# The recurrence's middle chunks beside other projections, and the diagonal layer's products in order of time

## The chip, the core and the metric

One Trainium2 chip, one of its cores. The metric is the device time of one execution in microseconds (us). Engines: TensorE (PE, with its weight loads PEld), VectorE (DVE), ScalarE (ACT), GpSimd (POOL) and SyncE (SP), whose one queue issues all DMAs of this kernel. Each engine takes its instructions in the order in which they stand in its queue.

## The reference

Two layers over two token groups, 128 context tokens and 2048 sample tokens, with D = 1024. All is float32. The first layer has two mixers side by side: a gated linear recurrence in four heads (HGRN2), in both directions, and a complex diagonal state space (S5) of 32 groups, also in both directions:

```
z = jnp.dot(h, w_in)                       # h: normalised and modulated tokens, 1024 -> 3584
q, f_fw, f_bw, v, g_a, u, g_b = jnp.split(z, EVEN_SPLITS, axis=-1)
S_t = diag(f_t) S_{t-1} + k_t v_t^T        # HGRN2, per head, forward and backward
o_t = S_t^T q_t
x_t = lbar * x_{t-1} + bb u_t              # S5, per group, forward and backward
y   = gelu(y_f + y_b + d_skip * u)
y   = y * sigmoid(y @ w_glu + b_glu)
out = concat(norm(o) * silu(g_a), y * silu(g_b)) @ w_out
```

The second layer is a gated short convolution between two projections. The outputs are all tokens after a last norm and the final states of the first layer.

## The kernel before

Tokens stand in the free dimension. They are cut into six tiles (five of 384, the last of 256) and these into three parts, `p0`, `p1` and `p2`, of two tiles each. A projection (`proj_all`, `proj_group`, `mm3`, L361) multiplies a 128x128 block of weights with a tile's `h`. Each operand is split into a high and a low half (`whi`, `wlo`, `hhi`, `hlo`), so one block takes 8 x 3 = 24 matmul passes into a PSUM tile `pj`. `load_w` loads a block by DMA, ACT casts it (L341), and DVE or POOL, in turns, makes `wlo` (L345). `make_h` norms a tile and writes its two halves; of these there are three pairs of buffers. `spill` evacuates `pj` and stores it to HBM: `zq`, `zff`, `zfb`, `zv` (from `qfv()`, the recurrence's inputs) and `zga`, `zgb` (from `gates()`).

The diagonal layer handles 16 tokens at a time: 136 blocks of 16 for 2176 tokens. `spill_u` stores its input to `u_d`; `s5_load_u` loads it as `su`, 128 partitions by 272 elements per group: for each block of 16 tokens two neighbouring elements, one for each half `hh`. `s5_in` (L602) multiplies `su` with the input matrices `psi`, which it first makes on DVE and POOL from loaded tables `pe` and `pb`, and copies the result (PSUM tile `lv`) into the state array `X` (L637, L638). `X` does not lie in order of time: block `c = 8 a + b` stands in group `b` at place `a`, so that `s5_scan` can run over 8 groups of 17. `s5_out` (L694) takes `X` out again (`sxm`, L711 and L712), builds its output matrices (`SO`, and `GS`, which goes through HBM and returns as `sM`) and accumulates in `lv`: `sM` with `su` (L717, L719) and `SO` with `sxm` (L722). Before, all these products have their columns in the order of `X`: the operand `su` is read as 8 runs of 17 at a step of 16 elements.

The recurrence handles chunks of 128 tokens, 17 of them. `hgrn_chunk` is a generator: it loads `hq`, `hff`, `hvf`, goes through seven levels of doubling blocks (products at L796, L820 and L822; decays on DVE and POOL at L826 and L828) and then updates the state `S` (L850 to L882). `hgrn_run` starts a chunk every 4 steps and so keeps three or so alive. Modulation rows (`mod_late`, L225) are issued beside them.

The program is put into order when it is built: a scheduler takes instructions by rank, the rank being the place in the program's text, and by when it reckons an operand to be ready. `rank(tc, n)` shifts the rank of what stands under it: a negative `n` puts it earlier. The result is a fixed order for each engine. Before, the second `hgrn_run` (chunks 6 to 11) stands ahead of `gates()` for `p1`, and `make_h` of both tiles of `p2` behind it.

Of the kernel before, what the change touches and what calls it, by code (L numbers as in the profile page):

```python
# [15 lines left out]
AF = mybir.ActivationFunctionType  # L16
OP = mybir.AluOpType
# [10 lines left out]
NC8 = NTOK // 8  # L28
NSAM = DEC // 8
NC16 = NTOK // 16  # L30
NS16 = DEC // 16
NG16 = NC16 // 8
# [17 lines left out]
MWB = 3  # L50
RX = 0
FU = 2
KPOOL = (1, 2, 4, 6)

PV = {}
# [8 lines left out]
def vw(t, off, dims):  # L64
    return bass.AP(t.tensor, t.offset + off, [list(t.ap[0])] + [list(d) for d in dims])


def raw_ap(t, off, dims):
    return bass.AP(t.tensor, t.offset + off, [list(d) for d in dims])
# [525 lines left out]
def s5_load_u(nc, g, p, g0):  # L595
    u = p.tile([128, 2, NC8], F32, name="su")
    for j in range(2):
        nc.sync.dma_start(u[:, j], raw_ap(g.u_d, (g0 + j) * 16 * 8 * NC8, [(NC8, 8), (8 * NC8, 16), (1, NC8)]))
    return u


def s5_in(nc, g, p, X):  # L602

    V, A, T, G = nc.vector, nc.scalar, nc.tensor, nc.gpsimd
    W = WX
    for r in range(8):
        G0 = 4 * r
        us = [s5_load_u(nc, g, p, G0 + 2 * q) for q in range(2)]
        SI = []
        for d in range(2):  # L610
            bt = p.tile([128, 2, 4, 2, 64], F32, name="pb", bufs=1)
            nc.sync.dma_start(bt.rearrange("p a g r q -> p a (g r q)"),
                              raw_ap(g.I["s5_bt"], d * 16 * 8192 + r * 1024, [(0, 8), (8192, 16), (1, 1024)]))
            for hh in range(2):
                e = p.tile([128, 4, 2, 64], F32, name="pe")
                nc.sync.dma_start(e.rearrange("p g r q -> p g (r q)"),
                                  raw_ap(g.et_d, ((d * 16 + 8 * (1 - hh)) * 32 + G0) * 128,
                                         [(32 * 128, 8), (0, 16), (1, 512)]))
                si = p.tile([128, 4, 2, 64], F32, name=f"psi{d}{hh}")
                tb = p.tile([128, 4, 2, 64], F32, name="ptb")  # L620
                V.tensor_tensor(si, vw(e, 0, [(128, 4), (0, 2), (1, 64)]), bt[:, 0], op=OP.mult)
                G.tensor_tensor(tb, vw(e, 64, [(128, 4), (0, 2), (1, 64)]), bt[:, 1], op=OP.mult)  # L622
                V.tensor_tensor(si[:, :, 0], si[:, :, 0], tb[:, :, 0], op=OP.subtract)
                V.tensor_tensor(si[:, :, 1], si[:, :, 1], tb[:, :, 1], op=OP.add)
                SI.append(si)
        for q in range(2):
            pr = 2 * r + q
            for j in range(2):
                P = g.ps_l.tile([128, 512], F32, name="lv")
                for d in range(2):  # L630
                    for hh in range(2):
                        T.matmul(out=P[:, d * NC16:(d + 1) * NC16],  # L632
                                 lhsT=SI[2 * d + hh][:, 2 * q + j].rearrange("p r q -> p (r q)"),
                                 rhs=vw(us[q], j * NC8 + hh, [(2, 8), (16, NG16)]), start=(hh == 0), stop=(hh == 1))
                o = slice(64 * j, 64 * j + 64)
                Pv = P[:, :2 * NC16].rearrange("p (d c) -> p d c", d=2)
                A.activation(vw(X[o], pr * W + NG16, [(32 * W - NG16, 2), (1, NC16)]), Pv[0:64], AF.Copy)  # L637
                V.tensor_copy(vw(X[o], (16 + pr) * W + NG16, [(32 * W - NG16, 2), (1, NC16)]), Pv[64:128])  # L638


def s5_powers(nc, g, p):
# [52 lines left out]
def s5_out(nc, g, p, X):  # L694
    V, A, T, G = nc.vector, nc.scalar, nc.tensor, nc.gpsimd
    W = WX
    todo = [s5_matrices(nc, g, p, pr) for pr in range(AH)]
    for pr in range(16):
        g0 = 2 * pr
        if pr + AH < 16:  # L700
            todo.append(s5_matrices(nc, g, p, pr + AH))
        so = todo.pop(0)
        u = s5_load_u(nc, g, p, g0)
        M = p.tile([128, 2, 384], F32, name="sM")
        for j in range(2):
            nc.sync.dma_start(M[:, j], raw_ap(g.gs_d, (g0 + j) * 16 * 496, [(16, 8), (496, 16), (1, 384)]))
        for j in range(2):
            gr = g0 + j
            o = slice(64 * j, 64 * j + 64)
            xm = p.tile([128, 2, NC16], F32, name="sxm")  # L710
            V.tensor_copy(xm[0:64], vw(X[o], pr * W, [(32 * W + NG16, 2), (1, NC16)]))  # L711
            A.activation(xm[64:128], vw(X[o], (16 + pr) * W, [(32 * W + NG16, 2), (1, NC16)]), AF.Copy)  # L712
            P = g.ps_l.tile([128, 512], F32, name="lv")
            for hh in range(2):
                po = P[:, hh * NC16:(hh + 1) * NC16]
                ue = [vw(u, j * NC8 + i, [(2, 8), (16, NG16)]) for i in range(2)]
                T.matmul(out=po, lhsT=M[:, j, 128:256], rhs=ue[hh], start=True, stop=False)  # L717
                c0 = 0 if hh == 0 else 256
                T.matmul(out=po, lhsT=M[:, j, c0:c0 + 128], rhs=ue[1 - hh], start=False, stop=False)  # L719
                for d in range(2):  # L720
                    e = 8 * hh + 1 - d
                    T.matmul(out=po, lhsT=so[d][:, j, e:e + 8].rearrange("p e o -> p (e o)"), rhs=xm[:, d],  # L722
                             start=False, stop=(d == 1))
            z = p.tile([128, NC8], F32, name="sz")
            y = p.tile([128, NC8], F32, name="sy")
            Pv = P[:, :NC8]
            A.activation(z, Pv, AF.Square)
            c2 = 2.0 * math.sqrt(2.0 / math.pi)
            V.tensor_scalar(z, z, 0.044715 * c2, c2, op0=OP.mult, op1=OP.add)
            V.tensor_tensor(z, z, Pv, op=OP.mult)  # L730
            A.activation(z, z, AF.Sigmoid)
            V.tensor_tensor(vw(y, 0, [(1, 2), (2, 8), (16, NG16)]), z.rearrange("p (h b a) -> p h b a", h=2, b=8),
                            Pv.rearrange("p (h b a) -> p h b a", h=2, b=8), op=OP.mult)
            nc.sync.dma_start(g.y_d[gr * 16:gr * 16 + 16].rearrange("o t c -> t o c"), y)


# [2 lines left out]
def hgrn_run(nc, g, cs, every, end=False):  # L739

    todo, t = list(cs), 0
    while todo or t % every or (end and g.live):
        if todo and t % every == 0:
            g.live.append(hgrn_chunk(nc, g, todo.pop(0)))
            next(g.side, None)
        for x in list(g.live):
            if next(x, None) is None:
                g.live.remove(x)
        t += 1


def hgrn_chunk(nc, g, c):
# [50 lines left out]
    for lvl in range(7):  # L803
# [21 lines left out]
        kv = vw(KK, 0, sp)  # L825
        (G if lvl in KPOOL else V).tensor_tensor(kv, kv, vw(tot, n + 1, [(-n - 1, 2), (2, nb), (0, h)]), op=OP.mult)  # L826
        qv = vw(QQ, 0, sp)
# [256 lines left out]
def kernel(ctx: ExitStack, tc: tile.TileContext, I, O, dram=None):  # L1084
    nc = tc.nc
    V, A, G, T = nc.vector, nc.scalar, nc.gpsimd, nc.tensor
    g = Ctx()
# [85 lines left out]
    def x_rstd(ti):  # L1173
        x = load_x(nc, g, ti, I["x"])
        return x, rstd_of(nc, g, x, TILES[ti][1] - TILES[ti][0])

    def make_h(ti, x_rs=None):
        x, rs = x_rs or x_rstd(ti)
        hs[ti] = norm_mod(nc, g, 0, ti, x, rs, hl_tiles(g))

    p0, p1, p2 = PARTS
# [9 lines left out]
    def us():  # L1191
        return [spill_u(nc, g, b) for b in range(4)]
# [10 lines left out]
    with tc.tile_pool(name="big0", bufs=1) as b0:  # L1203
        with tc.tile_pool(name="kt", bufs=1) as kt:
            g.KT = kt.tile([128, 8, 2, 2, 2, 16], F32, name="KT")
            g.K1 = kt.tile([128, 2, 2, 16], F32, name="K1")
            with tc.tile_pool(name="bigA", bufs=1) as bA:
                g.bigs = itertools.cycle((b0, bA))
                f0, f1 = p0[::-1]
                with tc.tile_pool(name="md", bufs=1) as md:  # L1210
# [9 lines left out]
                    make_h(f1, xr1)  # L1220
                proj_all(nc, g, us(), [f0, f1], hs, FU)
                s5_prep(nc, tc, g)
# [7 lines left out]
            with tc.tile_pool(name="s5x", bufs=1) as xp:  # L1230
                X = xp.tile([128, 2, 2, 16, WX], F32, name="sX")
# [12 lines left out]
        with ExitStack() as st:  # L1244
            hgrn_pools(st)
            g.mw = st.enter_context(tc.tile_pool(name="mw", bufs=1))
            g.side = mod_late(nc, g, [(0, 4), (0, 5)] + [(1, cg) for cg in range(6)])
            make_h(p1[1])
            hgrn_run(nc, g, range(6), 4)
            proj_all(nc, g, qfv(), p1, hs)  # L1250
            hgrn_run(nc, g, range(6, 12), 4)
            proj_all(nc, g, gates(), p1, hs)
            for ti in p2:
                make_h(ti)
            proj_all(nc, g, qfv(), p2, hs)
            hgrn_run(nc, g, range(12, 17), 4, True)
            for _ in g.side:
                pass
            Sb = g.hs.tile([128, 512], F32, name="hS", bufs=2)
            nc.sync.dma_start(Sb, I["state_hgrn"][1])  # L1260
            proj_all(nc, g, gates(), p2, hs, 1)
            wg = glu_weights(nc, g)
# [185 lines left out]
```

## Time and profile before

| | us |
|---|---|
| median of 3 runs | 2559.59 (2558.59 to 2570.24) |
| profiled execution | 2557.99 |
| its span | 2556.2 |
| PE busy | 2378.2 (93%) |
| DVE busy | 1377.8 (54%) |
| ACT busy | 988.2 (39%) |
| POOL busy | 682.9 (27%) |

PE is busy nearly throughout, so its idle time and its slow time are what there is to win, apart from work taken off it. Busy time of PE is counted from modelled ends and its passes overlap: a pass of 334 ns can stand 173 ns behind the one before. The pace of a stretch is therefore read from counts and distances, and from the granted clock (PEclk, 1.00 at 2.4 GHz, 0.50 at 1.2 GHz).

### The profile page before, as it was taken

What the parts mean: (1) busy time and instruction counts of PE and PEld (TensorE: products, weight loads), DVE (VectorE), ACT (ScalarE), POOL (GpSimd) and SP (SyncE); (2) the same over time, 40 slices, a digit from 0 to 9 for tenths busy, and PEclk for the clock granted to TensorE, in tenths of its full rate; (3) what the DMA queues carried; (4) which work ended last, traced back from release to release, by engine and by line L of the source; (5) the groups of instructions that cost most, each with busy time, mean ns of one, the idle gap of its engine ahead of it and who ended that gap; (6) DMA issues with size and microseconds to landing.
All of it is one profiled execution on the core that took longest, in us unless ns stands there. A gap on an engine that the chain in (4) does not pass through costs nothing.

```text
span 2556.2 us, 46638 instructions
## 1 busy us (share of the span) xinstructions
PE 2378.2 (93%) x18452; PEld 2266.5 (89%) x18452; DVE 1377.8 (54%) x2960; ACT 988.2 (39%) x1995; POOL 682.9 (27%) x740
## 2 busy tenths in 40 slices
PE   5999879999999877999989989999999999999997
PEld 3998779899887766998888989999999999899997
DVE  5975648955445787137767672234622244622234
ACT  3544212233345776256544342233422232422231
POOL 0334332332213332123322322222322222322220
PEclk8999989999999988999999999999999999999998
DMA  7577653354456652454698432233321223222221
GB/s 254 149 225 199 179 160 94 115 172 134 130 169 186 195 155 100 151 164 135 205 302 253 133 112 75 75 98 108 108 72 61 66 76 115 74 67 66 67 61 64
DMA packets 277418, 340.16 MB, mean 133 GB/s; under 512 B 79056, under 2 KB 221136, under 8 KB 277072
## 3 DMA queue, kind: packets, MB, share of 16 engines
q1 hardware_dynamic: 277200, 337.18, 43.3%
q8 instruction: 145, 2.38, 0.4%
q14 instruction: 73, 0.60, 0.1%
HBM read 265.18 MB, written 71.94 MB: 132 GB/s over the span
## 4 chain that ended last, share of the span: by engine, by line
PE 65%; DVE 6%; DMA 3%; ACT 3%; issue 2%; POOL 1%; SPq 0%; DVEq 0%; ACTq 0%; POOLq 0%
PE pj L361 56%; DMA hff<-zff 1%; PE lv L717 1%; PE lv L722 1%; PE lv L719 1%; DVE hQ L828 1%; PE lv L796 1%; PE nx L225 1%; DMA mwm<-in_w_mod 1%; PE ax L870 1%; DVE zst L982 1%; DVE hS L914 1%; PE ax L581 1%; PE ax L850 0%; POOL wlo L345 0%
## 5 line engine op out<-in xcount | busy, mean ns | idle before, releaser
L361 PE MATMUL pj<-hhi,whi 128*128 128x384 f32 (+1 forms) x3648 | 1179.9, 334 | 46.2 <-ACT hhi L303 26.5
L361 PE MATMUL pj<-hlo,whi 128*128 128x384 f32 (+1 forms) x3648 | 1178.4, 332 | 8.6 <-DVE hlo L304 6.0
L361 PE MATMUL pj<-hhi,wlo 128*128 128x384 f32 (+1 forms) x3456 | 1142.9, 331 | 1.3 <-POOL wlo L345 0.9
L361 PEld LDWEIGHTS pj<-hhi,whi 128*128 128x128 f32 x3648 | 691.9, 192 | 61.6 <-ACT hhi L303 28.1
L361 PEld LDWEIGHTS pj<-hlo,whi 128*128 128x128 f32 x3648 | 691.9, 191 | 15.5 <-DVE hlo L304 8.6
L345 POOL TENSOR_TENSOR wlo<-wraw,whi 128x256 fp32r<-128x256 f32 x472 | 383.5, 843 | 1058.2 <-ACT whi L341 1004.2
L361 PEld LDWEIGHTS pj<-hhi,wlo 128*128 128x128 f32 x3456 | 660.7, 191 | 4.8 <-POOL wlo L345 1.5
L341 ACT ACTIVATE whi<-wraw 128x512 fp32r<-128x512 f32 x472 | 271.7, 623 | 582.4 <-PE pj L361 383.2
L345 DVE TENSOR_TENSOR wlo<-wraw,whi 128x256 fp32r<-128x256 f32 x472 | 188.1, 456 | 133.7 <-ACT whi L341 133.7
L1053 DVE TENSOR_TENSOR ccg<-ccg,pj 128x384 f32<-128x384 f32 (+1 forms) x48 | 25.5, 531 | 250.8 <-PE pj L361 232.7
L993 DVE SCALAR_TENSOR_TENSOR xr<-pj,mod,xr 128x384 f32<-128x384 f32 (+2 forms) x152 | 77.2, 529 | 136.8 <-PE pj L361 122.8
L826 POOL TENSOR_TENSOR hK<-hK,ht 128x512 f32<-128x512 f32 x68 | 89.2, 1316 | 216.4 <-ACT hMg L810 152.7
L303 ACT ACTIVATE hhi<-nsq,mod 128x384 fp32r<-128x384 f32 (+2 forms) x144 | 74.7, 558 | 62.8 <-DVE nsq L301 62.5
L828 DVE TENSOR_TENSOR hQ<-hQ,ht 128x512 f32<-128x512 f32 x102 | 80.8, 807 | 18.2 <-PE lv L796 16.2
L632 PE MATMUL lv<-su,psi 128*128 128x136 f32 x256 | 65.3, 416 | 23.2 <-DVE sX L638 13.9
L282 DVE TENSOR_TENSOR nac<-nac,nsq 128x384 f32<-128x384 f32 (+1 forms) x112 | 70.2, 627 | 27.3 <-ACT nsq L281 25.1
L622 POOL TENSOR_TENSOR ptb<-pe,pb 128x512 f32<-128x512 f32 x32 | 53.0, 1665 | 112.2 <-DMA pb<-in_s_bt 80.2
L304 DVE SCALAR_TENSOR_TENSOR hlo<-nsq,mod,hhi 128x384 fp32r<-128x384 f32 (+2 forms) x144 | 82.2, 599 | 1.1 <-ACT hhi L303 1.1
L632 PEld LDWEIGHTS lv<-su,psi 128*128 128x128 f32 x256 | 53.7, 235 | 31.2 <-DVE sX L638 15.5
L391 ACT ACTIVATE zst<-pj 128x384 f32<-128x384 f32 (+1 forms) x96 | 44.3, 462 | 93.4 <-PE pj L361 46.7
L281 ACT ACTIVATE nsq<-xr 128x384 f32<-128x384 f32 (+1 forms) x84 | 41.9, 503 | 94.7 <-DVE xr L993 90.1
L1073 DVE TENSOR_TENSOR ccs<-ccs,pj 128x384 f32<-128x384 f32 (+1 forms) x48 | 25.4, 528 | 88.3 <-ACT ccs L1072 88.3
(299 smaller groups left out, 2847.0 us busy)
## 6 DMA issues: line engine op xcount, KB each, us to landing
wraw<-in_w_in_odd SPq DMA_DIRECT2D x96, 512.0 KB
wraw<-in_w_in_even SPq DMA_DIRECT2D x92, 512.0 KB
mwm<-in_w_mod SPq DMA_DIRECT2D x64, 256.0 KB
big<-in_x SPq DMA_DIRECT2D x10, 1536.0 KB
wraw<-in_w_out_even SPq DMA_DIRECT2D x24, 512.0 KB
wraw<-in_w_out_odd SPq DMA_DIRECT2D x24, 512.0 KB
su<-u_d SPq DMA_DIRECT2D x64, 136.0 KB
pb<-in_s_bt SPq DMA_DIRECT2D x16, 512.0 KB
```

What stands on the lines that cost most here:

```text
L282: e.tensor_tensor(acc, acc, sq[:, :n], op=OP.add)
L303: A.activation(hi[:, k, a:b], raw[:, a:b], AF.Identity, bias=sh)
L304: V.scalar_tensor_tensor(lo[:, k, a:b], raw[:, a:b], sh, hi[:, k, a:b].bitcast(F32), op0=OP.add, op1=OP.subtract)
L341: nc.scalar.activation(hi[:, i:i + ca], raw[:, i:i + ca], AF.Copy)
L345: e.tensor_tensor(lo[:, k], raw[:, k], hi[:, k].bitcast(F32), op=OP.subtract)
L361: nc.tensor.matmul(out=P[:, :n], lhsT=a[:, k, :], rhs=b[:, k, :n], start=(k == 0 and i == 0), stop=(k == kd - 1 and i == 2))
L391: nc.scalar.activation(st[:, :n], P[:, :n], AF.Copy)
L622: G.tensor_tensor(tb, vw(e, 64, [(128, 4), (0, 2), (1, 64)]), bt[:, 1], op=OP.mult)
L632: T.matmul(out=P[:, d * NC16:(d + 1) * NC16], lhsT=SI[2 * d + hh][:, 2 * q + j].rearrange("p r q -> p (r q)"), rhs=vw(us[q], j * NC8 + hh, ...
L826: (G if lvl in KPOOL else V).tensor_tensor(kv, kv, vw(tot, n + 1, [(-n - 1, 2), (2, nb), (0, h)]), op=OP.mult)
L828: V.tensor_tensor(qv, qv, vw(tot, 1, [(n - 1, 2), (2, nb), (0, h)]), op=OP.mult)
L993: nc.vector.scalar_tensor_tensor(x[:, a:e], P[:, a:e], g.mod[l][:, 16 + b, s:s + 1], x[:, a:e], op0=OP.mult, op1=OP.add)
```

## The change

Two things. In the diagonal layer, `su` is read in order of time, `[(2, 136)]` in place of `[(2, 8), (16, 17)]`. The copies into and out of `X` now do the rearrangement: they read or write the side that is in order of time in steps of 8. The order of the result `sy` becomes plain. In the program's order, the second `hgrn_run` moves behind `gates()` of `p1` and behind both `make_h` of `p2`, with the first of these ahead of the gates, and gets a rank 1000 earlier.

```diff
@@ s5_in
-                                 rhs=vw(us[q], j * NC8 + hh, [(2, 8), (16, NG16)]), start=(hh == 0), stop=(hh == 1))
+                                 rhs=vw(us[q], j * NC8 + hh, [(2, NC16)]), start=(hh == 0), stop=(hh == 1))
-                Pv = P[:, :2 * NC16].rearrange("p (d c) -> p d c", d=2)
-                A.activation(vw(X[o], pr * W + NG16, [(32 * W - NG16, 2), (1, NC16)]), Pv[0:64], AF.Copy)
+                Pv = P[:, :2 * NC16].rearrange("p (d a b) -> p d b a", d=2, b=8)
+                A.activation(vw(X[o], pr * W + NG16, [(32 * W - NG16, 2), (NG16, 8), (1, NG16)]), Pv[0:64], AF.Copy)
...
@@ s5_out
-            V.tensor_copy(xm[0:64], vw(X[o], pr * W, [(32 * W + NG16, 2), (1, NC16)]))
+            xv = xm.rearrange("p d (a b) -> p d b a", b=8)
+            V.tensor_copy(xv[0:64], vw(X[o], pr * W, [(32 * W + NG16, 2), (NG16, 8), (1, NG16)]))
...
-                ue = [vw(u, j * NC8 + i, [(2, 8), (16, NG16)]) for i in range(2)]
+                ue = [vw(u, j * NC8 + i, [(2, NC16)]) for i in range(2)]
...
-            V.tensor_tensor(vw(y, 0, [(1, 2), (2, 8), (16, NG16)]), z.rearrange("p (h b a) -> p h b a", h=2, b=8),
+            V.tensor_tensor(vw(y, 0, [(1, 2), (2, NC16)]), z.rearrange("p (h c) -> p h c", h=2),
...
@@ tile_hybrid_backbone_kernel
+RH = 1000
...
-            hgrn_run(nc, g, range(6, 12), 4)
+            make_h(p2[0])
             proj_all(nc, g, gates(), p1, hs)
-            for ti in p2:
-                make_h(ti)
+            make_h(p2[1])
+            with rank(tc, -RH):
+                hgrn_run(nc, g, range(6, 12), 4)
             proj_all(nc, g, qfv(), p2, hs)
```

On PE the order is the same until late in the first six chunks. Then, before, where chunk 5 begins, the sixth, counted from 0 (`lv` from `hq` and `hK`), PE's queue holds recurrence products (`lv`, `ax`) and modulation rows (`nx`) alone:

```order
L864 MATMUL ax<-eye,hK 128x128 x2
L796 MATMUL lv<-hQ,hMg 32x32 x16
L796 MATMUL lv<-hq,hK 32x32 x32
L864 MATMUL ax<-eye,hK 128x128 x2
L225 MATMUL nx<-mwm,silp 32x256 x2
L796 MATMUL lv<-hQ,hMg 32x32 x32
L870 MATMUL ax<-hv,hkT 128x128 x4
```

At the same place of the changed kernel (its lines are numbered one or two higher) projection passes of `p2` (`pj`) follow the chunk's first products:

```order
L866 MATMUL ax<-eye,hK 128x128 x4
L798 MATMUL lv<-hQ,hMg 32x32 x16
L798 MATMUL lv<-hq,hK 32x32 x32
L362 MATMUL pj<-hhi,whi 128x384
L362 MATMUL pj<-hlo,whi 128x384
L362 MATMUL pj<-hhi,wlo 128x384
```

What moved: projections of `qfv()` for `p2`, which before stand behind chunk 11, now stand between the products of chunks 5 to 11, and the modulation rows come later.

On POOL, towards the end of chunks 6 to 11, the queue of before holds decays of the recurrence (`hK`) and the clearing of `hAn` alone; the number of an `ht` tells one level's totals from another's:

```order
L826 TENSOR_TENSOR hK<-hK,ht_9389 128x2x128x2
L786 MEMSET hAn 128x128
L826 TENSOR_TENSOR hK<-hK,ht_9478 128x2x64x4
L826 TENSOR_TENSOR hK<-hK,ht_9451 128x2x4x64
L826 TENSOR_TENSOR hK<-hK,ht_9581 128x2x16x16
```

In the changed kernel splits of weights (`wlo`) stand between them:

```order
L828 TENSOR_TENSOR hK<-hK,ht_10158 128x2x64x4
L346 TENSOR_TENSOR wlo<-wraw,whi 128x256 x2
L828 TENSOR_TENSOR hK<-hK,ht_10131 128x2x4x64
L346 TENSOR_TENSOR wlo<-wraw,whi 128x256 x2
L828 TENSOR_TENSOR hK<-hK,ht_10261 128x2x16x16
```

What moved: the splits for these projections, which before follow chunk 11 in one run of 32, now come partly between the chunks' levels.

## Rows read from the trace of the kernel before

**Rows 1.** Stretch, length, busy PE, PEld, DVE, ACT, POOL (instructions), clock, DMA, GB/s

```profile
245.00:400.00 155.00, 131.83 (x622) 123.00 (x621) 85.21 (x147) 36.31 (x79) 51.53 (x38) 0.89 0.57 166
540.00:745.00 205.00, 203.10 (x1195) 184.20 (x1194) 100.11 (x213) 67.06 (x147) 48.42 (x49) 0.99 0.48 138
...
860.00:1000.00 140.00, 107.34 (x2574) 90.20 (x2574) 117.67 (x254) 107.98 (x229) 44.80 (x43) 0.88 0.49 148
...
1020.00:1120.00 100.00, 100.00 (x689) 94.05 (x690) 10.51 (x31) 27.20 (x56) 18.49 (x27) 1.00 0.51 159
1120.00:1240.00 120.00, 113.56 (x2008) 106.29 (x2008) 84.70 (x172) 80.72 (x165) 40.09 (x39) 0.97 0.46 140
```

**Rows 2.** Groups by shape, the diagonal layer's products: count, busy us, mean ns, idle before

```profile
L632 PE MATMUL lv<-su,psi 128*128 128x136 f32 x256 | 65.3, 416 | 23.2 <-DVE sX L638 13.9 <-DMA su<-u_d 4.8 <-DVE psi L624 4.4
L722 PE MATMUL lv<-sxm,SO 128*128 128x136 f32 x256 | 41.4, 284 | 0.0
L719 PE MATMUL lv<-su,sM 128*128 128x136 f32 x128 | 41.2, 410 | 0.0
L717 PE MATMUL lv<-su,sM 128*128 128x136 f32 x128 | 40.2, 403 | 1.9 <-DMA sM<-gs_d 1.8
```

**Rows 3.** Timeline of PE: start, length of the merged passes, engine, line, count

```profile
286.92 2.03 PE L632 MATMUL lv<-su,psi 128*128 128x136 f32 x8
...
600.94 0.62 PE L717 MATMUL lv<-su,sM 128*128 128x136 f32 x2
601.38 0.64 PE L719 MATMUL lv<-su,sM 128*128 128x136 f32 x2
601.85 0.64 PE L722 MATMUL lv<-sxm,SO 128*128 128x136 f32 x4
```

**Rows 4.** Line 796 in 768 to 769.5 and 773 to 773.8: min/median/max ns

```profile
L796 PE MATMUL lv<-hQ,hMg x32: 202/213/221, 768.3 to 769.0; 128*32 128x32 f32 x32
...
L796 PE MATMUL lv<-hQ,hMg x32: 193/196/218, 773.3 to 773.5; 128*32 128x32 f32 x32
```

**Rows 5.** Waits of PE and of DVE in 245 to 400: total, times, longest

```profile
PE lv L632 <- DVE sX L638: 13.9, 5, 3.9
...
DVE psi L621 <- DMA pb<-in_s_bt: 38.3, 9, 6.5
```

**Rows 6.** Copies: by shape (busy, mean ns), or by line (min/median/max ns)

```profile
L391 ACT ACTIVATE zst<-pj 128x384 f32<-128x384 f32 x80 | 38.5, 482 | 93.4 <-PE pj L361 46.7 <-issue 46.6
L638 DVE COPY sX<-lv 64x272 f32<-64x272 f32 x32 | 14.2, 442 | 8.5 <-ACT sX L637 7.8
...
L711 DVE COPY sxm<-sX x32: 293/297/742, 517.9 to 739.5; 64x272 f32<-64x272 f32 x32
...
L408 ACT ACTIVATE zst<-pj x16: 255/428/491, 73.9 to 218.0; 128x384 f32<-128x384 f32 x8, 128x128 f32<-128x128 f32 x4, 128x256 f32<-128x256 f32 x4
```

**Rows 7.** Busy time of line 796 alone by stretch: PE, PEld (passes), clock, DMA share, GB/s

```profile
768.00:860.00 92.00, 12.65 (x864) 10.28 (x864) 0.96 0.58 178
860.00:1000.00 140.00, 23.39 (x1683) 19.57 (x1687) 0.88 0.49 148
...
1120.00:1240.00 120.00, 15.69 (x1120) 12.69 (x1120) 0.97 0.46 140
```

**Rows 8.** The same of line 361 (projections)

```profile
860.00:1000.00 140.00, 13.25 (x51) 9.87 (x51) 0.88 0.49 148
...
1020.00:1120.00 100.00, 94.79 (x625) 90.75 (x626) 1.00 0.51 159
1120.00:1240.00 120.00, 65.54 (x408) 59.38 (x408) 0.97 0.46 140
```

**Rows 9.** Chain of work, in order of time: one of its blocks in the pure stretch

```profile
1027.52 7.14 PE pj L361 x48
1035.22 7.22 PE pj L361 x48
```

**Rows 10.** The page's groups: weight splits on POOL

```profile
L345 POOL TENSOR_TENSOR wlo<-wraw,whi 128x256 fp32r<-128x256 f32 x472 | 383.5, 843 | 1058.2 <-ACT whi L341 1004.2
```

More of the change, by code (lines that the diff above doesn't have):

```diff
@@ L633, in s5_in @@
                                  lhsT=SI[2 * d + hh][:, 2 * q + j].rearrange("p r q -> p (r q)"),
-                                 rhs=vw(us[q], j * NC8 + hh, [(2, 8), (16, NG16)]), start=(hh == 0), stop=(hh == 1))
+                                 rhs=vw(us[q], j * NC8 + hh, [(2, NC16)]), start=(hh == 0), stop=(hh == 1))
                 o = slice(64 * j, 64 * j + 64)
-                Pv = P[:, :2 * NC16].rearrange("p (d c) -> p d c", d=2)
-                A.activation(vw(X[o], pr * W + NG16, [(32 * W - NG16, 2), (1, NC16)]), Pv[0:64], AF.Copy)
-                V.tensor_copy(vw(X[o], (16 + pr) * W + NG16, [(32 * W - NG16, 2), (1, NC16)]), Pv[64:128])
+                Pv = P[:, :2 * NC16].rearrange("p (d a b) -> p d b a", d=2, b=8)
+                A.activation(vw(X[o], pr * W + NG16, [(32 * W - NG16, 2), (NG16, 8), (1, NG16)]), Pv[0:64], AF.Copy)
+                V.tensor_copy(vw(X[o], (16 + pr) * W + NG16, [(32 * W - NG16, 2), (NG16, 8), (1, NG16)]), Pv[64:128])
 def s5_powers(nc, g, p):
@@ L710, in s5_out @@
             xm = p.tile([128, 2, NC16], F32, name="sxm")
-            V.tensor_copy(xm[0:64], vw(X[o], pr * W, [(32 * W + NG16, 2), (1, NC16)]))
-            A.activation(xm[64:128], vw(X[o], (16 + pr) * W, [(32 * W + NG16, 2), (1, NC16)]), AF.Copy)
+            xv = xm.rearrange("p d (a b) -> p d b a", b=8)
+            V.tensor_copy(xv[0:64], vw(X[o], pr * W, [(32 * W + NG16, 2), (NG16, 8), (1, NG16)]))
+            A.activation(xv[64:128], vw(X[o], (16 + pr) * W, [(32 * W + NG16, 2), (NG16, 8), (1, NG16)]), AF.Copy)
             P = g.ps_l.tile([128, 512], F32, name="lv")
@@ L731, in s5_out @@
             A.activation(z, z, AF.Sigmoid)
-            V.tensor_tensor(vw(y, 0, [(1, 2), (2, 8), (16, NG16)]), z.rearrange("p (h b a) -> p h b a", h=2, b=8),
-                            Pv.rearrange("p (h b a) -> p h b a", h=2, b=8), op=OP.mult)
+            V.tensor_tensor(vw(y, 0, [(1, 2), (2, NC16)]), z.rearrange("p (h c) -> p h c", h=2),
+                            Pv.rearrange("p (h c) -> p h c", h=2), op=OP.mult)
             nc.sync.dma_start(g.y_d[gr * 16:gr * 16 + 16].rearrange("o t c -> t o c"), y)
```

## The prediction

> **What bounds the kernel now.** I read the page's totals first, then stretches of the program side by side, then the matmuls by shape, then the waits. TensorE (PE) is busy 2378.2 us of a span of 2556.2 us, so the question in every stretch is whether PE works at a full pace there, and if not, who holds it. Four stretches matter [rows 1]. In 245 to 400 us, the input side of the diagonal layer (`s5_in`), PE is busy 131.83 of 155 us at a granted clock of 0.89. In 540 to 745 us, its output side (`s5_out`), PE is busy 203.10 of 205: whatever shortens a product there shortens the run. In 860 to 1000 us the recurrence stands almost alone: PE 107.34 of 140 at 0.88, with VectorE (DVE) at 117.67. In 1020 to 1120 the reverse holds: PE is full with projections and DVE has 10.51 us of work in 100.
>
> **The products in order of time.** Lines 632, 717 and 719 read their moving operand `su` as 8 runs of 17 elements at a step of 16 floats (64 bytes); line 722 reads `sxm` contiguously. All four have the same shape, 128x136 in f32, and a product is recorded as two passes: 256 passes of L632, 128 of L717, 128 of L719, 256 of L722 [rows 2]. Their means already differ (416, 403 and 410 ns against 284), but matmuls overlap, so what counts is the distance from one start to the next. From the timeline [rows 3]: L717, two passes in 0.62 us with the last lasting 0.40, gives 0.22; L719, two in 0.64, gives 0.23; L632, eight in 2.03, gives (2.03 - 0.41)/7 = 0.23; L722, four in 0.64, gives (0.64 - 0.28)/3 = 0.12. A pass with the 64-byte step costs 0.105 to 0.11 us more than a contiguous one.
>
> The change gives all 512 passes a step of 2 floats (8 bytes). No operand of before has that step, so I bound it: no gain if it costs what 64 bytes cost, 0.105 to 0.11 us a pass if it costs what contiguous reading costs. The nearest rows are two bursts of the recurrence, equal but for the pattern of the moving operand [rows 4]: at 768.3 us (first level) the stream jumps 513 floats after every column and the passes have a median of 213 ns; at 773.3 us (second level) it jumps after every second column and has 196, which is also what the later levels with longer runs have. One jump for two columns is already free there. The new step is a much smaller one, so I take the contiguous pace. In a sentence of its own, the Trainium skill ("SBUF — State Buffer", Specifications (TRN2)) says that lines are 16 bytes and two hits in a line suffice for full bandwidth; by it an 8-byte step is at the contiguous pace, and the two bursts agree.
>
> For `s5_out` that is 256 x 0.105 = 27 us off a stretch in which PE has 2 us of slack [rows 1]. PE waits there once for `sM`; with PE faster the way from `GS` through HBM back to `sM` is late more often, and I leave 3 us for it: **24 us**.
>
> For `s5_in` it is 256 x 0.11 = 28 us of PE time, but PE is not what holds that stretch. DVE stands 38.3 us waiting for the load `pb` (one buffer), and PE stands 13.9 us behind the copies out of PSUM that DVE makes in between [rows 5]. What PE saves there is mostly waited for at the next product. It is not all lost, because loads and stores of that stretch queue behind PE on SP's single queue. Ends: 0 (the load loop sets the pace) and 28. I take **8**, nearer the first end, since 23 us of idle PE already stand there.
>
> The copies change their patterns too. L637 and L638 now read PSUM in steps of 8 columns; L711 and L712 write `sxm` in steps of 8 floats; L732 writes a plainer pattern than before. Row by row: ScalarE (ACT) evacuates a 128x384 tile read plainly in 482 ns (L391), and L408, which reads PSUM in steps of 8 columns, has 491 as its longest [rows 6]: no price. L711 (median 297 ns) might rise to the 442 of L638 [rows 6]: 32 x 0.15 = up to 5 us of DVE time, beside 100.11 busy of 205 [rows 1], so nothing; without that cover it would cost those 5. A rule that speaks against this part: the Trainium skill ("Advanced Engine Details and Errata", PSUM Cachelines) wants every two consecutive PSUM elements contiguous, at a loss otherwise for matmuls; if the copies of L637 and L638 doubled by it, 64 x 0.4 = 26 us (an estimate) would fall on ACT and DVE in `s5_in` and its 8 us would be gone. The L408 row does not show such a loss for a copy.
>
> **The recurrence beside projections.** A chunk has 224 passes at L796, so counts give its pace [rows 7]: 768 to 860 us: 864/224 = 3.9 chunks, 23.9 us each; 860 to 1000: 1683/224 = 7.5 chunks, 18.6 us each, with 51; 1120 to 1240: 5.0 chunks, 24.0 us each, with 408 [rows 8]. What PE itself needs for a chunk I take from the last: (113.56 - 65.54)/5.0 = 9.6 us [rows 1, 8]. So alone a chunk takes 18.6 us, of which PE needs 9.6: the rest is the chain between DVE, ACT, GpSimd (POOL) and PE. Beside projections it takes 24, but PE is then nearly full. Afterwards 1020 to 1120 us hold 625 recorded projection passes and no recurrence, at 48 passes per 7.7 us, 0.161 us each [rows 8, 9].
>
> The builder's order shows what moves. Counting every matmul of the recurrence's helper lines (160 per chunk), between the 600th and the 1708th (6.9 chunks) stood 44 projection passes, now 292: 248 move in from the pure stretch. Before: 6.9 x 18.6 = 128 us, and 248 x 0.161 = 40 us later, 168 together. After: the first 3.2 chunks (to the 1108th) still have only 68 passes, because the third part's second tile has no `h` yet: 59 us at the old pace. The other 3.75 chunks stand with 224: PE needs 36 + 36 = 72, the chain alone 70, and at the mixed pace of 24 it is 90; I take 84. Sum 143, a gain of **25**. Ends: 40 (the passes fit wholly into the chain's gaps) and 0 (each stands in front of a recurrence product and delays it by its length); below that by the slower rival. What comes with the passes is counted in the 24 us: weight splits on DVE and POOL, the casts and evacuations on ACT, the weight loads and `z` stores on SP among the chunk's own loads. The small modulation products (L225) that come later now move from one stretch that PE fills to another; I cost them at nothing. The rest of the order, from the GLU on, is almost the same.
>
> **Sum.** 24 + 8 + 25 = 57. The profiled execution took 2557.99 us (span 2556.2), which is 1.6 below the median of 2559.59, well within what the runs differ by. 2558 - 57 = **2501 us**.
>
> **Rivals.**
> - The 8-byte step is as slow as the 64-byte one. For it: no row has that step. Against: the two bursts [rows 4]. Then only the recurrence gains: 2558 - 25 = 2533.
> - The recurrence gains nothing, since its chain is delayed by all that is put in front of it. For it: 18.6 against 24 us per chunk [rows 7]. Against: 1120 to 1240 us, where mixing loses PE only 6.4 of 120 us [rows 1]. 2558 - 32 = 2526.
> - Both go fully: 27 + 28 + 40 = 95, 2463. For it: `s5_in` holds PE's clock down to 0.89 and SP's queue interleaves PE's stores with the loads; against: `pb`.
> - Slower. In POOL's queue the weight splits (843 ns each, [rows 10], in fours) now stand between the steps of a chunk's decay, and a step behind four of them is late by 3.4 us for all the live chunks, since DVE and PE take their work in order. With 248 passes (40 us), 20 splits on POOL (17) and 20 on DVE delaying more than one chunk each, the 6.9 chunks could take past 31 us each (214 us): a loss of 45, which outweighs the diagonal layer's 32 by 13. Then 2571 or more. From 31 us per chunk this decides; no stretch of before shows more than 24.
> - The change does nothing that shows: the step not free and the mixing neutral: about 2557.
>
> **Chances.** Forecast (2480 to 2520) 0.55; the recurrence gains nothing 0.16; both go fully 0.14; the step not free 0.08; nothing shows 0.04; slower 0.03. About 0.5% (12.8 us) is what a measurement of this kernel can tell from no change. The first four cases lie below 2547, except for the edge of the fourth: faster 0.92, within 0.05, slower 0.03. The range reaches from the case in which both go fully to past the fourth: 2463 to 2538.
>
> **What would show it.** In the changed profile L632, L717 and L719 have means near 284 ns instead of 403 to 416; about 410 would mean the first rival. `s5_out` has the same pairs in some 180 us instead of 205, with more PE waits for `sM`. `s5_in` shows nearly its 155 us with PE less busy and its clock not higher; if it shrinks below 140, the load loop was not the bound. Chunks 6 to 11 show projection passes among L796's, at 19 to 24 us per chunk; past 31 the slower rival is right. A pure stretch remains, shorter by some 40 us. The forecast is wrong if any stretch after the recurrence (from the GLU on) changes by more than a few us, since nothing of it is changed.

## The result, and the profile after

| | before, us | changed, us |
|---|---|---|
| median of 4 runs each | 2563.2 (2558.59 to 2570.24) | 2525.41 (2521.9 to 2527.22) |
| profiled execution | 2557.99 | 2521.9 |
| its span | 2556.2 | 2520.1 |

The ratio is 0.9849, with a 95% interval from 0.982 to 0.9877: 38.7 us faster (32 to 46). The forecast was 57 us and a time of 2501. The stated range, 2463 to 2538, holds the result; the narrower band that the forecast gave itself among the chances, 2480 to 2520, does not hold the median of 2525. (0.9849 of the 2558 us that the forecast started from is 2519, at the band's upper edge.) Beside the other kernels on another chip (`e8_after_again` below) the same kernel has 0.9852.

I read the groups by shape first, since the forecast names what they should show (a line's number is one or two higher than in [rows 2, 6]):

```profile
L633 PE MATMUL lv<-su,psi 128*128 128x136 f32 x256 | 47.8, 344 | 37.1 <-DVE sX L639 21.3 <-DMA su<-u_d 7.0 <-DVE psi L622 4.4
...
L724 PE MATMUL lv<-sxm,SO 128*128 128x136 f32 x256 | 40.0, 278 | 0.0
...
L719 PE MATMUL lv<-su,sM 128*128 128x136 f32 x128 | 26.5, 288 | 7.2 <-DMA sM<-gs_d 5.9 <-DVE sy L734 1.1 <-DVE SO L571 0.2
L721 PE MATMUL lv<-su,sM 128*128 128x136 f32 x128 | 25.7, 282 | 0.0
L714 ACT ACTIVATE sxm<-sX 64x272 f32<-64x272 f32 x32 | 23.2, 725 | 1.2 <-DVE sX L669 0.4
...
L713 DVE COPY sxm<-sX 64x272 f32<-64x272 f32 x32 | 17.4, 544 | 42.6 <-PE lv L724 42.2
L639 DVE COPY sX<-lv 64x272 f32<-64x272 f32 x32 | 14.2, 442 | 4.5 <-ACT sX L638 3.8
```

The two `sM` products are at the pace of the contiguous one (288 and 282 ns against 278; [rows 2] had 403 and 410). The input product L633 has a mean of 344, though its median is 282 (410 before): the mean mixes passes at two levels of the clock. Four bursts of 16 passes show it, two of before (L632) and two of the changed kernel (L633), as stretches with the line's own busy time (columns as in [rows 7]):

```profile
308.16:312.14 3.98, 3.97 (x16) 3.19 (x16) 1.00 0.43 115
321.11:325.17 4.06, 4.06 (x16) 3.73 (x16) 0.50 0.62 127
```

```profile
321.78:325.78 4.00, 3.99 (x16) 3.67 (x16) 0.50 0.58 131
370.03:372.23 2.20, 2.20 (x16) 1.99 (x16) 1.00 0.64 181
```

With the 64-byte step a burst takes 4 us at either level; with the 8-byte step it takes 2.2 us at 2.4 GHz and still 4 at 1.2 GHz. Over the whole stretch the median from start to start was 233 ns at both levels before, and is now 120 ns at 2.4 GHz and 227 at 1.2 GHz. So a pass gains 113 ns at the upper level and 6 at the lower, and 94 of the 256 ran at the lower one (in front of the two bursts at 0.50 PE had stood idle for 3.8 us each). Hence the group's busy time fell by 17.5 us (65.3 to 47.8). Its idle time rose by 13.9 us, from 23.2 to 37.1: most of what PE saved there it now waits for.

The copy out of PSUM in steps of 8 columns (L639) costs 442 ns as before [rows 6]. The copies that write `sxm` in steps of 8 floats are dearer, 544 ns on DVE and 725 on ACT, and PE does not wait for them. Before, these two were:

```profile
L712 ACT ACTIVATE sxm<-sX 64x272 f32<-64x272 f32 x32 | 13.7, 430 | 0.8
L711 DVE COPY sxm<-sX 64x272 f32<-64x272 f32 x32 | 11.7, 366 | 50.0 <-PE lv L722 49.8
```

The timeline of PE in the output side (start, length, line, count) gives the distance from pass to pass:

```profile
587.49 0.40 PE L719 MATMUL lv<-su,sM 128*128 128x136 f32 x2
587.73 0.40 PE L721 MATMUL lv<-su,sM 128*128 128x136 f32 x2
587.97 0.62 PE L724 MATMUL lv<-sxm,SO 128*128 128x136 f32 x4
```

Four `sM` passes take 587.97 - 587.49 = 0.48 us, 0.12 each, where [rows 3] gave 0.22 and 0.23. From the first to the last `sM` product of the output side it is now 182.1 us (538.4 to 720.5) against 204.8 (540.8 to 745.6).

Stretches of the changed kernel (columns as in [rows 1]): input side, output side, the recurrence with projections, and what is left of projections alone:

```profile
245.00:400.00 155.00, 117.93 (x628) 113.36 (x627) 86.35 (x148) 36.46 (x79) 52.51 (x38) 0.83 0.61 165
538.00:725.00 187.00, 179.80 (x1226) 165.92 (x1225) 104.41 (x215) 76.88 (x151) 47.74 (x48) 1.00 0.54 155
824.00:1000.00 176.00, 152.67 (x2968) 133.13 (x2955) 140.10 (x294) 130.96 (x269) 57.51 (x53) 0.94 0.53 163
1000.00:1067.00 67.00, 67.00 (x473) 64.23 (x472) 9.71 (x24) 19.48 (x43) 14.33 (x19) 1.00 0.44 137
```

In the input side PE is less busy and its granted clock lower, 0.83. The recurrence's own line in the third stretch, to count its pace by:

```profile
824.00:1000.00 176.00, 25.36 (x1784) 20.79 (x1770) 0.94 0.53 163
```

1784/224 = 8.0 chunks, 22.1 us each, with 344 projection passes beside them.

### The profile page after: what moved, and what is told of

Read it like the earlier page. It is cut to its first block, busy times and chain, and to the rows that moved or that the text cites. A ratio compares the mean times of both kernels' runs of the same rounds, so it can differ in the third digit from the quotient of the medians.

```text
span 2520.1 us, 46630 instructions
## 1 busy us (share of the span) xinstructions
PE 2336.8 (93%) x18452; PEld 2235.7 (89%) x18452; DVE 1384.5 (55%) x2960; ACT 992.5 (39%) x1991; POOL 686.9 (27%) x740
## 5 line engine op out<-in xcount | busy, mean ns | idle before, releaser
L1055 DVE TENSOR_TENSOR ccg<-ccg,pj 128x384 f32<-128x384 f32 (+1 forms) x48 | 25.5, 532 | 248.5 <-PE pj L362 233.0
L633 PE MATMUL lv<-su,psi 128*128 128x136 f32 x256 | 47.8, 344 | 37.1 <-DVE sX L639 21.3
L633 PEld LDWEIGHTS lv<-su,psi 128*128 128x128 f32 x256 | 43.2, 238 | 41.6 <-DVE sX L639 23.2
```

Source lines behind the costliest of these rows:

```text
L633: T.matmul(out=P[:, d * NC16:(d + 1) * NC16], lhsT=SI[2 * d + hh][:, 2 * q + j].rearrange("p r q -> p (r q)"), rhs=vw(us[q], j * NC8 + hh, ...
```

## The experiments

**The parts one by one.** `e1_diag_only` takes the new order back, `e2_order_only` makes it alone; `e3_out_only` and `e4_in_only` split the diagonal layer's part.

```diff
 e1: the changed kernel with
-            make_h(p2[0])
+            hgrn_run(nc, g, range(6, 12), 4)
             proj_all(nc, g, gates(), p1, hs)
-            make_h(p2[1])
-            with rank(tc, -RH):
-                hgrn_run(nc, g, range(6, 12), 4)
+            for ti in p2:
+                make_h(ti)
 e2: before, with the reverse of these lines
 e3: e1, with L633, L638 and L639 as before
 e4: before, with L633, L638 and L639 as changed
```

> The diagonal layer's change alone, with the recurrence in its old place. Theory (the two parts add up, and the diagonal layer's gain is kept to the end): the first stretches end as in the changed kernel, so about -25 us against before at the first transposes of the recurrence, and the same -25 at the end: ratio about 0.990. Rival (the recurrence's stretch, bound by its loads and its chain, gives part of it back): -15 or less at the end. Rival (most of the change comes from the order): within 5 us of before.

> The new place of the recurrence's middle chunks alone, with the diagonal layer as before. Theory (the mixing wins some 24 us up to chunk 12, and 12 to 14 of it are lost again in the last five chunks): -10 to -12 us at the end, ratio about 0.9957, with chunk 12 some 22 us early. Rival (the forecast's term, 25 us, holds and the loss after chunk 12 comes of the diagonal layer's faster end): -25, ratio 0.990. Rival (the order gains nothing): within 3 us of before.

> The diagonal layer's output side alone in order of time, its input side and the recurrence as before. Theory: 205 us become some 183, -22 us at the end, ratio about 0.9915. Rival (the output side gains less when the input side is slow, because both share a resource): under -15.

> The diagonal layer's input side alone in order of time. Theory (the loads and the copies out of PSUM set the pace of that stretch): -2 us (0 to -4), ratio 0.999, with PE's idle time before these products up by 14 us or so and its clock lower, not higher. Rival (the forecast's middle value): -8, ratio 0.997. Rival (PE's time sets it): -28.

| | median, us | ratio to before | 95% interval | us, from the ratio |
|---|---|---|---|---|
| before (17 runs) | 2555.28 | | | |
| e1, diagonal layer | 2531.3 | 0.9912 | 0.9892 to 0.9932 | -22 |
| e2, order | 2536.75 | 0.9931 | 0.9904 to 0.9957 | -18 |
| e3, output side | 2538.64 | 0.9936 | 0.9917 to 0.9954 | -16 |
| e4, input side | 2551.26 | 0.9986 | 0.9973 to 0.9999 | -4 |

Both parts gain. The diagonal layer gives 22 us where 32 were forecast, most of it by its output side (16); the input side gives 4, an interval of 0.3 to 6.9, so the forecast's 8 lies outside and 28 far outside. In e4 PE's idle time before the input products is 38.6 us against 23.2 [rows 2], as the theory wanted (its group, columns as there):

```profile
L632 PE MATMUL lv<-su,psi 128*128 128x136 f32 x256 | 48.5, 347 | 38.6 <-DVE sX L638 20.3 <-DMA su<-u_d 10.2 <-DVE psi L624 4.9
```

The order gives 18 us, 11.0 to 24.5: more than the 10 to 12 that I expected; the forecast's 25 lies just outside, and that it gains nothing is excluded. The pieces of the new order (the earlier `make_h`, the new place of the second `hgrn_run`, its rank) were not tried apart.

**The changed kernel again, the pace of the input side, the modulation rows, the steps.**

```diff
 e5
-            bt = p.tile([128, 2, 4, 2, 64], F32, name="pb", bufs=1)
+            bt = p.tile([128, 2, 4, 2, 64], F32, name="pb", bufs=2)
-                si = p.tile([128, 4, 2, 64], F32, name=f"psi{d}{hh}")
+                si = p.tile([128, 4, 2, 64], F32, name=f"psi{d}{hh}", bufs=2 - d * hh)
 e6, in hgrn_run; g.ns is 2 from the first chunk
-            next(g.side, None)
+            for _ in range(g.ns):
+                next(g.side, None)
 e7
-                                 rhs=vw(us[q], j * NC8 + hh, [(2, NC16)]), ...
+                                 rhs=vw(us[q], 0, [(8, NC16 // 2), (1, 2)]), ...
-                             rhs=ue[hh], start=True, ...
+                             rhs=vw(u, 0, [(3, NC16)]), start=True, ...
-                             rhs=ue[1 - hh], start=False, ...
+                             rhs=vw(u, 0, [(4, NC16)]), start=False, ...
```

> The changed kernel once more, beside the others on one chip, so that the parts can be added up. Theory (the parts add up): the ratios of the two parts alone, 0.9912 and 0.9931, multiply to 0.9844; so 0.984 to 0.985. Rival (the recurrence gives back part of the diagonal layer's gain when both are there, as the profiled executions read one by one would have it: -28 and -27 against -36): 0.986 to 0.988.

> The changed kernel with two buffers for the table pb in the diagonal layer's input side (one of the tables psi gives up its second buffer to make room). Theory (DVE's wait for pb, 53 us, is the loop that sets the pace of that stretch): the stretch of 155 us becomes 10 to 20 us shorter, 2503 to 2515 us where the changed kernel has 2520 to 2525, and DVE's wait for pb falls below 20 us. Rival (another load or the copies out of PSUM take the place of pb): within 4 us of the changed kernel, with the wait moved to them. Rival (loads that start earlier delay PE's stores): slower by some us.

> The changed kernel with two steps of modulation rows per chunk from the start in place of one, so that none is left for the last five chunks. Theory (some 12 us given back after chunk 12 come from the 48 modulation passes, 5.4 us of PE, and the waits for their weights): the last five chunks take 6 to 9 us less, while the first chunks, where PE has idle time, pay 0 to 4: -3 to -9 us against the changed kernel. Rival (the giving back comes from the recurrence's own products and the projections, which stand there in larger number): the last five chunks stay as long as they are, 0 to +4 us at the end. Rival (the modulation's products are wanted as filler and their weight loads collide with the chunks' loads early on): +5 or more.

> The changed kernel with other steps of the moving operand in the diagonal layer, reading other elements of the same tile: the first sM product a step of 12 bytes, the second 16 bytes, the input product pairs of neighbours at a step of 32 bytes. Its output is that of other data. Theory (a pass is as fast as contiguous reading while two elements of a 16-byte line are used in succession, as the Trainium skill has it): 12 bytes costs part of the 0.11 us (mean between 284 and 403 ns), 16 bytes the whole (about 400 ns, 0.23 us from pass to pass), pairs nothing (s5_in mean as in the changed kernel). Rival (any small step is free, and 64 bytes is too large): all three near 284 ns. Rival (only a step of 8 bytes or less is free): 12 bytes the whole too, and the pairs dearer.

| | median, us | ratio to before | 95% interval |
|---|---|---|---|
| before (11 runs) | 2554.34 | | |
| e8, changed kernel again | 2514.87 | 0.9852 | 0.9833 to 0.987 |
| e5, two `pb` | 2514.05 | 0.9853 | 0.9834 to 0.9872 |
| e6, modulation early | 2537.24 | 0.9927 | 0.991 to 0.9943 |

e8: the parts' product is 0.9844, the measured ratio 0.9852, so the two parts add up within what can be measured.

e7 settles the step. It reads other elements than the reference asks for, so its output is that of other data; it ran once (2531.91 us), and only the length of its passes is used. These are its groups:

```profile
L633 PE MATMUL lv<-su,psi 128*128 128x136 f32 x256 | 47.9, 340 | 35.9 <-DMA su<-u_d 16.6 <-DVE psi L625 8.3 <-DVE nsq L302 5.1
...
L721 PE MATMUL lv<-su,sM 128*128 128x136 f32 x128 | 41.9, 417 | 0.0
L719 PE MATMUL lv<-su,sM 128*128 128x136 f32 x128 | 33.7, 348 | 0.1
```

A step of 16 bytes (L721) costs as much as 64 bytes did, 12 bytes (L719) lies between, and neighbours in pairs, 32 bytes from pair to pair (L633), cost no more than the 8-byte step. From start to start, as medians over the trace, at a granted clock of 1.00 or nearly: 115 ns contiguous, 120 to 123 at 8 bytes, 172 at 12, 233 at 16, 233 at 64 (L719 of before), 123 for pairs (those at the upper level). The Trainium skill ("SBUF — State Buffer", Specifications (TRN2)) asks for two hits in a 16-byte line for full bandwidth; these passes agree with it.

e5: DVE's largest wait in the input side, as the changed kernel has it and as e5 has it (in 245 to 400 and 232 to 387 us: total, times, longest):

```profile
DVE psi L622 <- DMA pb<-in_s_bt: 43.5, 9, 6.2
```

```profile
DVE psi L622 <- DMA pe<-et_d: 36.9, 13, 8.4
```

The wait for `pb` is gone and `pe` has taken its place (14.9 us in the changed kernel). From the first input product to the last it is 137.4 us instead of 149.7 in e8, and the first `sM` product comes 13.4 us sooner (525.2 against 538.6). So the `pb` loop did set the pace of that stretch, until `pe` took over. But the time at the end is the same. In the profiled executions 10.4 us of the 13.4 are left at the GLU's first product and 2.0 at the end. Among the unchanged stretches that lie between, one looks like this near its start in e5 and like this in e8 (same work, 40 us from 5 us behind the start of each):

```profile
1780.00:1820.00 40.00, 37.28 (x199) 36.53 (x198) 19.82 (x37) 14.64 (x26) 11.39 (x14) 0.91 0.20 66
```

```profile
1789.00:1829.00 40.00, 38.51 (x220) 37.99 (x219) 19.14 (x35) 15.37 (x27) 11.37 (x14) 1.00 0.21 66
```

The granted clock is at the lower level for part of the 40 us in e5 (0.91), and 21 passes fewer run. This stretch is 5.5 us longer in e5 (243.8 against 238.3), the next of its kind 3.7.

e6: slower than the changed kernel by 22 us in the medians, a loss of the size that the third theory expected; that weight loads collide, its reason, was not looked into. The last five chunks did become shorter (below), by more than the first theory had. But the built order changed too: beside the fifth to ninth chunk's worth of the recurrence's products (L798, L822, L824) the trace of e8 has 155 projection passes and that of e6 has 48, and the stretch of projections alone grew from 94.9 to 128.9 us.

**The last five chunks.** Counted in the profiled executions, in us (lines of the changed kernel): from the first chunk's transposes (L774) to the last of chunk 11's, to the first of chunk 12's, to the state update of chunk 12 (L884; chunk 0 has none), to the GLU's first product (L978). A chunk's transposes stand at its start, so chunks 10 and 11 are finished only behind chunk 12's transposes:

| | chunks 0 to 11 | then, nearly alone, projections | to chunk 12's state | to the GLU |
|---|---|---|---|---|
| before | 224.1 | 154.7 | 49.8 | 61.4 |
| e1, order of before | 223.6 | 152.5 | 46.4 | 60.8 |
| e2, new order | 248.6 | 95.0 | 63.3 | 62.4 |
| e8, new order | 255.7 | 94.9 | 63.6 | 59.8 |
| e6 | 249.1 | 128.9 | 53.3 | 59.0 |
| e10 | 259.0 | 102.7 | 59.5 | 63.3 |

Two kernels were to tell what gives time back after chunk 12's transposes, and one to take all three findings together:

```diff
 e9, in glu; RG is 1000
-            nc.sync.dma_start(rw[:, b, :, o:o + m], ...)
+            with rank(g.tc, -RG if t0 == 0 else 0):
+                nc.sync.dma_start(rw[:, b, :, o:o + m], ...)
 e10, behind the second hgrn_run
+            for _ in g.side:
+                pass
             proj_all(nc, g, qfv(), p2, hs)
 e11: e5, e9 and e10 together
```

> The changed kernel with the loads of the GLU's first tile (hlo from y_d) issued 1000 ranks earlier, so that no store stands between them in SP's queue. Theory (the GLU's first product waits 4 to 6 us for ACT's hhi because these loads stand behind stores whose data come late): the wait falls to 1 or 2 us and the GLU starts 3 to 5 us sooner after chunk 12's transposes (119 us instead of 123); at the end -2 to -5 us. Rival (the buffer hlo comes free too late for an earlier issue): no change, within 2 us.

> The changed kernel with the modulation rows that are left after chunk 11 issued at once there, in the stretch of projections alone, in place of one step with each of the last five chunks; everything before that stretch keeps its order. Theory (what the modulation costs the last five chunks is its 5.4 us of PE and 3 to 4 us of waits for its weights; among projections alone it costs the same 5.4 us of PE): from chunk 12's transposes to the GLU's first product 112 to 115 us instead of 123, the stretch before it 6 us longer, and -3 to -4 us at the end. Rival (the last five chunks are longer because more of the chunks' own work stands there): 123 us stay and the end is +5 or so. Rival (the projections wait for the modulation's weights too): the stretch before it 10 us longer, 0 at the end.

> The changed kernel with all three: two buffers for pb, the GLU's loads early, the modulation's rest among projections alone. Theory (the three add up, and the stretches after the GLU keep their length): -13 - 3 - 4 = -20 us against the changed kernel, a ratio to before of 0.977 to 0.979. Rival (what is won before the GLU is given back after it, as with pb alone, where the granted clock fell to about 0.9 at the start of stretches with the same instructions): -5 to -10 us, 0.981 to 0.983. Rival (nothing is kept): 0.985.

| | median, us | ratio to before | 95% interval |
|---|---|---|---|
| before (11 runs) | 2557.64 | | |
| e9, GLU's load early | 2524.19 | 0.9868 | 0.9843 to 0.9893 |
| e10, modulation among projections | 2530.93 | 0.989 | 0.9869 to 0.9912 |
| e11, all | 2526.18 | 0.9881 | 0.9859 to 0.9903 |

e9: no gain; PE's wait for the GLU's input stays. The stores between the eight loads are gone, but the first load starts no sooner: 117.6 us behind chunk 12's transposes, 117.7 in e8. So the theory falls. The rival's number fits, but its reason (the buffer) is not shown: right before these loads SP waits 3.1 us for a store of `zga`, and no wait for their buffer shows.

```profile
PE pj L980 <- ACT hhi L971: 4.4, 1, 4.4
```

e10 fells my theory that the modulation rows cost the last five chunks their time. First the four stretches of e1 and of e8, then the last two of e10 (columns as in [rows 1]), then PE's waits in these two:

```profile
728.00:951.60 223.60, 190.52 (x3740) 161.70 (x3739) 163.80 (x348) 157.20 (x317) 68.86 (x68) 0.90 0.57 173
951.60:1104.10 152.50, 142.00 (x1327) 130.35 (x1325) 52.36 (x117) 64.91 (x137) 35.28 (x41) 0.97 0.47 150
1104.10:1150.50 46.40, 44.15 (x897) 40.79 (x901) 37.10 (x80) 33.69 (x70) 14.44 (x15) 1.00 0.55 162
1150.50:1211.30 60.80, 58.82 (x1066) 55.25 (x1063) 43.00 (x86) 38.37 (x83) 23.85 (x21) 1.00 0.41 123
```

```profile
727.10:982.80 255.70, 224.59 (x4039) 194.19 (x4038) 191.41 (x400) 181.92 (x370) 78.46 (x78) 0.94 0.57 175
982.80:1077.70 94.90, 94.90 (x905) 89.96 (x904) 25.87 (x58) 38.43 (x81) 22.03 (x28) 1.00 0.47 148
1077.70:1141.30 63.60, 59.73 (x1078) 52.30 (x1075) 43.32 (x90) 37.05 (x77) 20.26 (x18) 0.95 0.57 175
1141.30:1201.10 59.80, 53.89 (x1004) 50.51 (x1002) 42.08 (x84) 38.62 (x84) 25.77 (x25) 0.99 0.42 118
```

```profile
1089.00:1148.50 59.50, 54.20 (x1042) 50.12 (x1043) 43.18 (x87) 38.68 (x79) 22.36 (x22) 0.97 0.45 137
1148.50:1211.80 63.30, 52.78 (x989) 49.54 (x987) 41.80 (x84) 35.97 (x79) 22.33 (x21) 0.96 0.38 113
```

```profile
PE ax L852 <- ACT hAT L845: 10.3, 3, 5.0
PE pj L978 <- ACT hhi L969: 5.1, 1, 5.1
```

Without the modulation PE is 6.6 us less busy than in e8 over the two, and the two last just as long (122.8 against 123.4): idle time takes its place, 15.8 us, nearly all of it behind the chunks' chain (`hAT`) and the GLU's load. The last stretch has 59 to 63 us in all six kernels, whatever PE does in it, busy for 58.8 us (e1) or for 52.8 (e10). At the end e10 is slower than the changed kernel by 0.4%, a loss as the first rival expected (the intervals of the two just touch), so there is no sign that the modulation rows were badly placed beside the last chunks.

e11 keeps nothing of what it was to add up: 0.9881 against 0.9852 is rather a loss, of 0.3%, though the two intervals overlap. Its first `sM` product comes 8.0 us sooner than e8's (530.6), its chunk 12 6.3 us later (1084.0 against 1077.7), which would fit the loss of e10's edit outweighing e5's gain; which of the three did it was not tried further.

**A further buffer.** `e12_pe3` gives `pe` a third one:

```diff
 e12, against e5
-                e = p.tile([128, 4, 2, 64], F32, name="pe")
+                e = p.tile([128, 4, 2, 64], F32, name="pe", bufs=3)
-                si = p.tile([128, 4, 2, 64], F32, name=f"psi{d}{hh}", bufs=2 - d * hh)
+                si = p.tile([128, 4, 2, 64], F32, name=f"psi{d}{hh}", bufs=2 - d)
```

> The changed kernel with two buffers for pb and three for the tables pe in the diagonal layer's input side (two of the tables psi give up their second buffer). With pb doubled alone that stretch became 13 us shorter, DVE then waited 37 us for pe, and the end was the same. Theory (SP's queue stands behind the two pe buffers, so a third lets the loads run ahead): 3 to 8 us more than with pb alone, 16 to 21 us less than the changed kernel up to the GLU; at the end anything from 0 to -20 us, since the stretches after the GLU differ by up to 10 us between executions of the same instructions with their granted clock; if the loss there was chance, the ratio to before is 0.977 to 0.980. Rival (the products psi with one buffer now wait for PE, or the loads themselves are the bound): no more than with pb alone, 0.985.

Its median is 2507.07 us (before, 9 runs: 2557.0), a ratio of 0.9811 with an interval of 0.979 to 0.9832, the fastest of all. The reason I gave for it is not borne out: the input products take as long as in e5 (136.7 us against 137.4), and DVE still waits for `pe` (in 235 to 390 us):

```profile
DVE psi L622 <- DMA pe<-et_d: 38.2, 10, 10.2
```

Its last input product starts 8.2 us sooner than e8's (389.4 against 397.6), but its first `sM` product later (541.3 against 538.6), and its output side, from the first `sM` product to the last, takes 175.2 us instead of 184.2. Here the built order differs: 20 projection passes that stand in the output side of e8 stand in front of it in e12, which explains a part of this (in the pure stretch of before a pass took 0.161 us). It is ahead of e8 by 5.8 us at the first chunk's transposes, by 14.4 at chunk 12's and by 11.5 at the end, the chunks 0 to 11 taking 247.0 us instead of 255.7. Whether the loads or the order did that stays open.

## Why the prediction was right, and where it was off

- **The products in order of time: right in mechanism and size.** An 8-byte step runs at the contiguous pace; forecast were 0.105 to 0.11 us a pass, measured are 233 - 120 = 113 ns (the input product at the upper clock level) and 233 - 120 = 113 and 215 - 123 = 92 (the two `sM` products). The first rival (2533) falls. What the forecast did not see is that at the lower level the 64-byte step had next to no price (233 - 227 = 6 ns).
- **`s5_out`, 24 us: right or a little large.** 22.7 in the profile (204.8 to 182.1; in that of e3 to 185.2, so 19.6); e3's ratio says 16 (12 to 21). I left 3 us for a late `sM`; PE waits 5.9 for it now.
- **`s5_in`, 8 us: the reason right, the size too large.** 2.4 us in the profile (the first `sM` product at 538.4 instead of 540.8), 4 in e4. The loop of `pb` held that stretch, as e5 shows by lifting it; 13.9 us of what PE saved appear as more idle time before L633, and the clock fell from 0.89 to 0.83. The upper end was too large by itself: PE's busy time fell by 17.5 us and not by 28, since 94 passes ran at the lower level. The lower end, 0, was the better value.
- **The copies at nothing: right for the time.** The read of PSUM is unchanged (442 ns). The write of `sxm` rose on DVE by about what I allowed, and on ACT from 430 to 725 ns, which I had not priced.
- **The recurrence, 25 us: this term failed, by what it left out.** Measured by e2 it is 18 (11 to 24.5). Its own sum, 15 us more with projections beside the chunks and 40 less afterwards, came out as 32.1 more (255.7 against 223.6, e8 and e1) and 57.6 less (94.9 against 152.5): -25.5 at chunk 12's transposes, at 22.1 us per mixed chunk where 24 were reckoned. That this is the forecast's 25 is partly luck: with the diagonal layer as before (e2 and before) the same two come to 24.5 more and 59.7 less, -35.2. The step that failed is that nothing changes behind them: from there to the GLU forecast were 0, measured 16.2 us more (123.4 against 107.2). The records show what the 25.5 leaves out. Up to chunk 12's transposes e8 has 123 fewer on PE than e1 (4944 against 5067; 72 of them the recurrence's, 48 modulation rows), so work is still owed there. The next stretch has 181 more (1078 against 897; 15.6 us), about 123 from in front and 62 from behind. The last stretch has those 62 fewer (4.9 us) and is shorter by only 1: PE, full there in e1 (2.0 us idle), now waits (5.9). e2 against before gives back nearly as much there, 14.5 us (125.7 against 111.2). Net, -9.3 us between e8 and e1 and -20.7 between e2 and before, single executions each; -18 in e2's ratio. That the modulation products cost nothing there was, by e10, not the error.
- **The rival "the recurrence gains nothing" gives 2526, the median is 2525, and it is wrong all the same:** e2 alone excludes it. Its total fits because the diagonal layer gave 22 instead of 32 and the recurrence 18 instead of 0. In the same way the range from 2463 to 2538 holds the result without proving the sum: it was wide enough for four of the six cases.
- **Slower, from 31 us per chunk:** 22.1 measured; POOL's splits between the decays did not decide.
- **After the GLU nothing changes: right.** From its first product to the end of the span it is 1315.9 us before and 1313.3 after, and 1311.4 to 1320.7 in all fourteen profiled executions. So a few us between two single executions mean little; the ratios over several runs decide.

That the last chunks' chain, with the GLU's load, holds that stretch at 60 us is read from PE's waits and from the six lengths; it was not tried by making the chain itself shorter, so why it takes 60 us stays open.

## What to carry to other kernels

Work that fills a chain's gaps is taken from somewhere: count what stands beside the later chain-bound stretches too, since a stretch that a chain holds hardly shrinks when its filler leaves (here by 1 us for 4.9 us of PE's work). A stretch with idle time on the fast engine gains from a faster product only what the loop that holds it allows, so find that loop first (here a second `pb` buffer shortened the stretch by 12 us, though not the whole run). A price per pass that was read at one clock level need not hold at the other. A total that fits a rival's number proves nothing until the parts have been run alone.

## What was not expected

- The step of a moving operand in f32 has a graded price: 115 ns per pass of 136 columns when contiguous, 120 to 123 at 8 bytes, 172 at 12, 233 at 16 and no more at 64; pairs of neighbours at 32 bytes cost what 8 bytes cost (e7). That is at 2.4 GHz. At 1.2 GHz the input product took 227 ns at 8 bytes and 233 at 64.
- A copy from SBUF to SBUF that writes with a step of 32 bytes is dearer by 69% on ACT (725 ns; 430 before) and by 42% on DVE in the median (422; 297 before; the means, 544 and 366, hold a few copies of up to 1301 and 742 ns), while reading PSUM in such steps was free (442 both times).
- Stretches with the same instructions differ between executions: the one shown under e5 took 238.3 us in e8, 239.0 in e1 and 243.8 in e5, with clocks of 1.00, 0.94 and 0.89 in its first eighth. A gain of a few us early in the program can be lost, or not, at such places.
